# Moving the emission of the second half of the long-range attention behind two output projections

## The chip, the cores and the metric

The kernel runs on one core of a Trainium2 chip. A core has a matrix engine (PE, with its weight loads shown apart as PEld), a vector engine (DVE), a scalar engine (ACT), a general engine (POOL) and a queue engine (SP, SyncE) that here issues every DMA; sixteen DMA engines carry the transfers between the core's memory and the chip's main memory. The metric is the device time of one execution in microseconds, as the median of several runs; lower is better.

## What is computed

One layer of a hybrid encoder over a prompt of 2048 tokens and 32 sample tokens, with 1024 features. Two groups of attention heads work side by side: group A is a long-range differential attention over all earlier chunks, group B looks only at a band of nine chunks.

```
qa, ka, va, qb, kb, vb = split(rmsnorm(x) @ w_in)
oa = diff_attn(qa, ka, va)       # group A, 4 heads, chunk-causal over all keys
ob = band_attn(qb, kb, vb)       # group B, 8 heads, band of 9 chunks
h  = x + concat(rmsnorm(oa), rmsnorm(ob)) @ w_out
h  = h + relu(rmsnorm(h) @ w_up)**2 @ w_down
y  = rmsnorm(h + sigmoid(h @ w_gate) * (p @ w_proj))
```

Everything is float32. Each product is made of three matmuls in a reduced format: an operand is split in a high part (a rounded copy, made on ACT) and a low part (the rest, made on POOL or DVE), and the products high-high, high-low and low-high are summed (`mm3`, L216 to L222). `split` and `wunit` (L179 to L208) do this for each weight tile: a DMA load of 512 KB into `wr`, a copy on ACT into `wh`, a subtraction on POOL into `wl`.

## The kernel before

The tokens are cut in four blocks, 0 to 3: three of 512 and a last one of 544. Work is emitted in this order: the input projections; the first half of the group A attention (`attn_a` for the query pairs in `JA0`); the band attention (`attn_b`) in two parts; then, in `run` (from L1389), the stage around the change:

- the normalisation and the load of the attention output of block 0 (`onorm`, `oload`);
- the second part of the group A attention, `attn_a` for `JA1 = [(4, 5), (6, 7, 8)]`, that is, query pairs 4 to 7 and the sample tokens, whose outputs are read only by blocks 2 and 3;
- the output projection of block 0 (`outproj(0, ...)`), woven with the normalisation and load of block 1;
- the output projection of block 1, woven with the normalisation of block 0 for the MLP (`norms`, `cnorm`);
- the MLP of block 0, the MLP of block 1, the gate of block 1, and then everything for blocks 2, 0 and 3.

`outproj` (from L917) loops over eight column tiles d. Each d loads a weight tile of `w_out` (through `wunit`), loads a 256 KB tile `hd` of the input, makes 24 matmuls into `ops`, adds them to `hd` on DVE (L935), squares `hd` on ACT into `tmp` (L940) and stores `hd` to the scratch tensor `hS`. The tiles `hd`, `tmp`, `oraw` of `oload` and `tmp` of `cnorm` share one ring of four buffers, so that a load waits until an older tile is stored or used up. `cnorm` (from L945) reads `hS` back, scales it on DVE (L957) and splits it into `cH` and `cL`, the operands of the first MLP matmuls (`ups`).

`attn_a` (from L549) loops over four heads g. For each it loads a query tile (two DMAs for `q`), the keys (`ka`, for `JA1`'s first item two tiles in four DMAs) and a bias tile (`ba`), then works on each query pair of the item; a second pair has a `q` of its own. The loads of the first head need buffers of pools that are free once the input projections are done. The working tiles of `attn_a` lie where those of `attn_b` lay, and both use the same PSUM rings in the order in which they are emitted, so its computation comes after the last band attention.

No order is written out by hand for the engines. A list scheduler orders the instructions when the program is built: it keeps a timeline of its own, and gives each engine the earliest emitted instruction among those that are ready. What is emitted earlier thus goes first wherever both are ready, and what is emitted later fills the gaps. On the chip, each engine, SP among them, works through the list so made; an instruction that waits holds up those behind it. `tc.issue_after(x)` adds an edge that places what the block emits on x's engine behind x in that engine's list; it is an order of issue and no wait for x to end.

Of the kernel before, what the change touches and what calls it, by code (L numbers as in the profile page):

```python
# [76 lines left out]
JA1 = [(4, 5), (6, 7, 8)]  # L77
# [7 lines left out]
def drain(gen):  # L85
    for _ in gen:
        pass
# [13 lines left out]
def weave(main, side, step, i=0, n=1):  # L101
    for _ in main:
        if i % step == 0:
            for _ in range(n):
                next(side, None)
        i += 1
    drain(side)
# [37 lines left out]
class Kern:  # L145
# [44 lines left out]
    def wunit(self, src, shape, hi_eng="act", lo_eng="pool", pool=None):  # L190
        nc = self.nc
        if pool is None:
            raw = self.rawp.tile([P] + shape, F32, bufs=2, name="wr")
        else:
            raw = pool.tile([P] + shape, F32, tag="wr0", bufs=4, name="wr0")
        self.dma(raw, src)
        if self.pieces is not None:
            n = shape[0] // 2
            parts = []
            for x in range(2):  # L200
                parts.append(self.piece([n] + shape[1:]))
                self.split(*parts[x], raw[:, n * x : n * x + n], hi_eng, lo_eng)
            return tuple(Parts([p[i] for p in parts], n) for i in range(2))
        if pool is None:
            hi = self.wp.tile([P] + shape, F32R, tag="wh", bufs=3, name="wh")
            lo = self.wp.tile([P] + shape, F32R, tag="wl", bufs=3, name="wl")
        else:
            hi = pool.tile([P] + shape, F32R, tag="wh0", bufs=4, name="wh0")  # L208
            lo = pool.tile([P] + shape, F32R, tag="wl0", bufs=4, name="wl0")
        self.split(hi, lo, raw, hi_eng, lo_eng)  # L210
        return hi, lo
# [1177 lines left out]
    def run(self):  # L1389
        tc, nc, a = self.tc, self.nc, self.a  # L1390
        with ExitStack() as top:

            def opened(stack, name, bufs, space=None, side="left"):
                kw = {} if space is None else {"space": space}
                return stack.enter_context(
                    tc.tile_pool(name=name, bufs=bufs, side=side, reuse_waits="tile", **kw)
                )
# [17 lines left out]
            ps_o = opened(psx, "pso", 1, PSUM, "right")  # L1415
# [91 lines left out]
            self.qpool = opened(sq_, "ak", 1)  # L1507
            mz = mm
            sy = Rings((ps_s, "s"), (ps_t, "tp"), (ps_s, "s"), (ps_t, "tp"))
            with ExitStack() as x:  # L1510
                pool = opened(x, "a1", 1, side="right")
                self.kpool = Rings((self.qpool, "ka"), (self.qpool, "ka"), (Lean(pool, 1), "ka"))
                for js in JA1:
                    self.attn_a(js, pool, sy, sy, ps_o)
            self.nt = 4
            acc, cn, st = {}, {}, {}
            def norms(b, act, ps):
                self.colnorm(acc[b][0], b, 1.0 / D, wk, ps, "mm", self.rS)
                yield
                yield from self.cnorm(b, wk, act, cn)  # L1520
# [10 lines left out]
                        next(g, None)  # L1531
            drain(g)
            weave(self.outproj(1, wk, oa[1], mm, acc[1]), norms(0, actq, mm), 1, 1)
            up = Sized(opened(top, "uh", 20, side="right"), BLK)
            oxs = ExitStack()
            ox = opened(oxs, "ox", 1, side="right")
# [143 lines left out]
```

## Time and profile before

| what | value |
|---|---|
| median of 3 runs | 3037.97 us |
| lowest, highest | 3032.81, 3038.74 us |
| the profiled execution, its own time | 3036.97 us |
| span from its first to its last instruction | 3035.2 us |
| PE busy | 2936.1 us (97% of the span) |
| PEld, DVE, ACT, POOL busy | 85%, 60%, 58%, 62% |
| DMA moved | 528.50 MB, mean 174 GB/s |
| mean granted TensorE clock | 0.989 |

The profiled execution took 1.77 us more than its span, which is what lies around the first and the last instruction, and it ran 1.00 us under the median. A row of the timeline has its start, its duration, the engine, the line and the operation, and in brackets the idle time before it with what ended it. A row of the windows view has, for a stretch, the busy time of each engine with the number of instructions started (x), then the granted clock, the busy share of the DMA engines, and GB/s.

### The profile page before, as it was taken

The numbers are of one execution on the slowest core, as the hardware profiler recorded it, in microseconds if no ns is written. First come the engines' busy times: TensorE is split into PE (matmuls) and PEld (weight loads), VectorE is DVE, ScalarE is ACT, GpSimd is POOL, SyncE is SP. The second block draws the span as 40 slices with busy tenths as digits, with TensorE's granted clock in tenths as the row PEclk, the third lists the DMA queues.
The fourth block names the chain that finished last, engine by engine and source line by source line (L and its number), as shares of the span: only waits on it lengthen the run. The fifth ranks groups of instructions, "written<-read, shape, count | busy, mean of one in ns | idle before, by whom it ended". The sixth has DMA issues, their size and how long they took to land. (4 is left out here: it accounts for less than half of the span.)

```text
span 3035.2 us, 50381 instructions
## 1 busy us (share of the span) xinstructions
PE 2936.1 (97%) x17409; PEld 2590.1 (85%) x17409; DVE 1825.3 (60%) x4233; ACT 1746.3 (58%) x3234; POOL 1886.8 (62%) x2509
## 2 busy tenths in 40 slices
PE   7999999999999999999999999999899999999997
PEld 6788889999877888888888888779788888999997
DVE  5157564666655555666665666445677885677664
ACT  5256554777766665655565656454655555555455
POOL 3467775323456444756555655777687889787774
PEclk9999999999999999999999999999999999999999
DMA  9778766887877452645644443436433446323221
GB/s 310 263 223 247 238 226 208 264 245 216 247 250 220 149 158 84 197 151 160 210 135 138 143 146 103 160 137 229 154 108 119 153 142 240 127 91 119 100 101 54
DMA packets 297496, 528.50 MB, mean 174 GB/s; under 512 B 36557, under 2 KB 161521, under 8 KB 297241
## 3 DMA queue, kind: packets, MB, share of 16 engines
q1 hardware_dynamic: 297240, 525.28, 54.6%
q8 instruction: 138, 2.26, 0.3%
q14 instruction: 118, 0.96, 0.1%
HBM read 424.66 MB, written 104.45 MB: 174 GB/s over the span
## 5 line engine op out<-in xcount | busy, mean ns | idle before, releaser
L177 POOL TENSOR_TENSOR wl<-wr,wh 128x256 fp32r<-128x256 f32 x648 | 490.0, 789 | 241.5 <-ACT wh L182 224.0
L182 ACT ACTIVATE piece<-wr 128x512 fp32r<-128x512 f32 x406 | 245.9, 625 | 288.6 <-PE ups L221 136.8
L177 POOL TENSOR_TENSOR piece<-wr,piece 128x256 fp32r<-128x256 f32 x404 | 336.4, 860 | 91.2 <-ACT piece L182 83.9
L182 ACT ACTIVATE wh<-wr 128x1024 fp32r<-128x1024 f32 x228 | 240.4, 1056 | 195.9 <-PE ups L221 37.3
L167 POOL TENSOR_TENSOR wl<-wr,wh 128x256 fp32r<-128x256 f32 x264 | 203.1, 803 | 197.9 <-ACT wh L182 197.6
L220 PE MATMUL dps<-uh,piece 128*128 128x272 f32 (+1 forms) x768 | 246.6, 325 | 7.9 <-ACT piece L182 4.2
L167 POOL TENSOR_TENSOR piece<-wr,piece 128x256 fp32r<-128x256 f32 x280 | 238.0, 886 | 18.4 <-ACT piece L182 15.0
L222 PE MATMUL dps<-uh,piece 128*128 128x272 f32 (+1 forms) x768 | 247.1, 324 | 0.7 <-POOL piece L167 0.4
L221 PE MATMUL dps<-ul,piece 128*128 128x272 f32 (+1 forms) x768 | 247.5, 324 | 0.0
L220 PE MATMUL ups<-cs,piece 128*128 128x256 f32 (+1 forms) x864 | 245.5, 284 | 0.0
L222 PE MATMUL ups<-cs,piece 128*128 128x256 f32 (+1 forms) x864 | 245.5, 284 | 0.0
L221 PE MATMUL ups<-cs,piece 128*128 128x256 f32 (+1 forms) x864 | 245.3, 284 | 0.0
L220 PE MATMUL qps<-aH,wh 128*128 128x512 f32 (+1 forms) x640 | 226.2, 353 | 1.5 <-DVE ql L476 1.5
L221 PE MATMUL qps<-aL,wh 128*128 128x512 f32 (+1 forms) x640 | 226.7, 354 | 0.0
L222 PE MATMUL qps<-aH,wl 128*128 128x512 f32 (+1 forms) x640 | 226.3, 354 | 0.0
L639 ACT ACTIVATE e<-e,nm 128x128 f32<-128x128 f32 (+16 forms) x136 | 157.2, 1156 | 105.3 <-DVE nm L637 105.0
L1121 DVE TENSOR_TENSOR h<-h,dps 128x512 f32<-128x512 f32 x256 | 173.4, 682 | 70.2 <-PE dps L222 68.8
L1164 DVE TENSOR_TENSOR h<-h,dps 128x272 f32<-128x272 f32 (+1 forms) x384 | 189.0, 513 | 42.4 <-PE dps L222 42.0
L220 PE MATMUL dps<-uh,wh 128*128 128x512 f32 x512 | 205.5, 401 | 4.2 <-DVE h L1121 4.0
L220 PE MATMUL ups<-cH,wh 128*128 128x512 f32 x512 | 203.2, 398 | 3.5 <-ACT cH L182 3.5
L222 PE MATMUL ups<-cH,wl 128*128 128x512 f32 x512 | 202.8, 396 | 0.0
L221 PE MATMUL ups<-cL,wh 128*128 128x512 f32 x512 | 202.6, 396 | 0.0
(311 smaller groups left out, 9219.2 us busy)
## 6 DMA issues: line engine op xcount, KB each, us to landing
wr<-w_up SPq DMA_DIRECT2D x128, 512.0 KB, 3.5
wr<-w_down SPq DMA_DIRECT2D x128, 512.0 KB, 3.5
v<-vSa SPq DMA_DIRECT2D x64, 512.0 KB, 4.9
q<-qS SPq DMA_DIRECT2D x128, 256.0 KB, 5.6
wr<-w_qk SPq DMA_DIRECT2D x50, 512.0 KB, 5.3
ka<-kS SPq DMA_DIRECT2D x32, 512.0 KB, 8.6
wr<-w_out SPq DMA_DIRECT2D x32, 512.0 KB, 4.8
wr<-w_ple_gate SPq DMA_DIRECT2D x32, 512.0 KB, 3.5
```

Of the source, the lines that this page charges most:

```text
L167: nc.gpsimd.tensor_tensor(out[:, sl], a[:, sl], b[:, sl], op=op)
L177: nc.gpsimd.tensor_tensor(out[:, sl], a[:, sl], b[:, sl], op=op)
L182: nc.scalar.activation(hi, raw, AF.Copy)
L220: nc.tensor.matmul(ps, lh, rh, start=start and i == 0, stop=False)
L221: nc.tensor.matmul(ps, lh, rl, start=False, stop=False)
L222: nc.tensor.matmul(ps, ll, rh, start=False, stop=stop and i == n - 1)
L639: nc.scalar.activation(row, row, AF.Exp, bias=nmx, accum_out=z[:nr, m : m + 1])
L1121: nc.vector.tensor_tensor(hv, hv, ps, op=ALU.add)
L1164: nc.vector.tensor_tensor(hv, hv, ps, op=ALU.add)
```

## The change

The block that emits `attn_a` for `JA1` moves from ahead of `outproj(0)` to behind `outproj(1)`, and so behind the work woven with both. In the order of emission it is still ahead of the MLPs. Its instructions on SP, loads and stores, are placed behind the last weight load that was issued by `wunit`, for which `wunit` now keeps the load in `self.load`; at that point it is the load of `w_out`'s tile d = 7 for block 1.

```diff
-        self.dma(raw, src)
+        self.load = self.dma(raw, src)
...
             sy = Rings((ps_s, "s"), (ps_t, "tp"), (ps_s, "s"), (ps_t, "tp"))
-            with ExitStack() as x:
-                pool = opened(x, "a1", 1, side="right")
-                self.kpool = Rings((self.qpool, "ka"), (self.qpool, "ka"), (Lean(pool, 1), "ka"))
-                for js in JA1:
-                    self.attn_a(js, pool, sy, sy, ps_o)
             self.nt = 4
...
             weave(self.outproj(1, wk, oa[1], mm, acc[1]), norms(0, actq, mm), 1, 1)
+            with ExitStack() as x:
+                pool = opened(x, "a1", 1, side="right")
+                self.kpool = Rings((self.qpool, "ka"), (self.qpool, "ka"), (Lean(pool, 1), "ka"))
+                with tc.issue_after(self.load.ins):
+                    for js in JA1:
+                        self.attn_a(js, pool, sy, sy, ps_o)
             up = Sized(opened(top, "uh", 20, side="right"), BLK)
```

## The prediction

> **What bounds the kernel now.** I read the page first, then the windows view in five stretches, then in tens of microseconds where the first view loses something, then PE's waits there, and last the timelines of SP, DVE, ACT and PE around the longest wait.
>
> ```profile
> span 3035.2 us, 50381 instructions
> PE 2936.1 (97%) x17409; PEld 2590.1 (85%) x17409; DVE 1825.3 (60%) x4233; ACT 1746.3 (58%) x3234; POOL 1886.8 (62%) x2509
> ```
> ```profile
> 800.00:1000.00 200.00, 185.27 (x868) 151.22 (x868) 112.73 (x317) 127.83 (x239) 109.90 (x157) 0.95 0.78 237
> 1000.00:1900.00 900.00, 894.26 (x4607) 753.09 (x4606) 544.65 (x1383) 548.04 (x905) 500.13 (x708) 1.00 0.49 147
> ```
>
> PE is busy for 97% of the span, so the time is PE's work plus what PE loses. The change removes no matmul and adds none. From 1000 to 1900 us, where the moved attention is computed beside the MLPs, PE idles 900 - 894.3 = 5.7 us at clock 1.00; there is next to nothing to gain there. From 800 to 1000 us, the two output projections and the start of the MLP, it idles 14.7 us at clock 0.95. That stretch decides.
>
> ```profile
> 820.00:830.00 10.00, 10.00 (x50) 8.28 (x50) 6.74 (x22) 8.29 (x17) 6.27 (x11) 1.00 1.04 234
> 830.00:840.00 10.00, 9.87 (x52) 8.18 (x50) 1.77 (x7) 2.23 (x5) 3.81 (x7) 1.00 1.08 269
> 840.00:850.00 10.00, 5.52 (x13) 4.29 (x14) 3.78 (x12) 5.83 (x10) 6.91 (x10) 0.67 0.75 260
> 850.00:860.00 10.00, 10.00 (x50) 8.39 (x50) 5.80 (x14) 6.98 (x12) 7.47 (x11) 0.99 0.75 220
> ...
> 870.00:880.00 10.00, 7.21 (x25) 5.53 (x24) 6.08 (x18) 6.63 (x13) 5.26 (x8) 0.70 0.74 243
> ...
> 910.00:920.00 10.00, 10.00 (x51) 8.42 (x50) 6.09 (x13) 4.18 (x9) 8.55 (x11) 1.00 0.68 200
> 920.00:930.00 10.00, 10.00 (x52) 8.28 (x51) 3.14 (x11) 6.06 (x11) 5.04 (x9) 1.00 1.03 295
> 930.00:940.00 10.00, 8.44 (x40) 6.46 (x40) 6.20 (x14) 6.70 (x13) 9.91 (x14) 1.00 0.60 194
> 940.00:950.00 10.00, 8.89 (x40) 6.11 (x38) 5.54 (x14) 5.36 (x10) 5.36 (x7) 1.00 1.01 331
> 950.00:960.00 10.00, 6.77 (x25) 4.87 (x26) 5.26 (x18) 5.49 (x12) 1.86 (x2) 0.80 1.05 273
> 960.00:970.00 10.00, 9.95 (x42) 7.97 (x41) 6.01 (x17) 9.41 (x19) 6.84 (x11) 0.86 0.45 140
> ```
> ```profile
> PE ops L220 <- ACT wh L182: 4.6, 1, 4.6
> PE ups L220 <- ACT cH L182: 3.5, 2, 2.4
> PE ops L220 <- DMA oraw<-oT: 2.5, 1, 2.5
> ```
>
> Count matmuls, not busy time: behind an idle stretch the clock is low and matmuls last longer, which busy time hides. An undisturbed ten microseconds (850 to 860) start 50, so one is worth 0.20 us. By that measure there are three holes:
>
> - **Hole 1**, 840 to 850: 13 matmuls, 37 short: 7.4 us, for 4.48 us of idle time.
> - **Hole 2**, 870 to 880: 25 short: 5.0 us.
> - **Hole 3**, 930 to 970: 147 of 200, 53 short: 10.6 us, for 40 - 34.05 = 5.95 us of idle time, so 1.78 us lost for each idle one.
>
> The low clock behind a hole is in these prices. The Trainium skill ("TensorE: Matmul & The Clock Gate", Part 1) has the clock halved after an idle window of about 3.4 us and restored after as long a busy one; by that rule hole 1 would cost 4.6 + 1.7 = 6.3 us, and hole 2, idle for 2.8 us, need not throttle at all. The row of 870 to 880 grants 0.70 after the shorter idle time, so I go by the counted matmuls; with the rule's price in both places the sum below would be lower by 0.7 us.
>
> **What makes hole 1.** SP's list before it, and what its loads do to others:
>
> ```profile
> 818.10 2.93 SPq L158 DMA_DIRECT2D q<-qS  x4
> 821.20 0.48 SPq L158 DMA_DIRECT2D bb<-dbb  x1
> 821.72 2.54 SPq L158 DMA_DIRECT2D ka<-kS  x4
> 824.31 0.59 SPq L158 DMA_DIRECT2D ba<-dba  x1
> 825.14 0.57 SPq L158 DMA_DIRECT2D q<-qS  x1
> 826.61 0.37 SPq L158 DMA_DIRECT2D vbt<-vSb  x1
> 827.54 2.43 SPq L158 DMA_DIRECT2D q<-qS  x1
> 830.17 1.45 SPq L158 DMA_DIRECT2D hS<-hd  x2
> 833.87 0.34 SPq L158 DMA_DIRECT2D hd<-x_t  x1
> ```
> ```profile
> 841.35 0.69 DVE L935 TENSOR_TENSOR hd<-hd,ops 128x512 f32<-128x512 f32 x1 [6.78 <-DMA hd<-x_t]
> ```
>
> Nine of these DMAs are the first head of the moved attention: two `q` of the four at 818.10 (the other two belong to the band attention), four `ka`, one `ba`, and the two `q` at 825.14 and 827.54. The sizes in the page's list of DMA issues (`q` 256 KB, `ka` two of 512 and two of 256, `ba` 128) give 2688 KB, 2.75 MB. At the 234 and 269 GB/s of the rows from 820 to 840, where the DMA engines are full (1.04, 1.08), that is 2.75 MB / 251 GB/s = **10.9 us of all DMA engines**, and SP issues nothing of the projection between 818 and 830. Two stores of `hd` wait behind them, then `hd<-x_t` for d = 2. It goes at 833.87, and DVE gets it at 841.35, 7.5 us later. The same load after the burst:
>
> ```profile
> hd<-x_t SPq DMA_DIRECT2D x1, 256.0 KB, 2.9
> ba<-dba SPq DMA_DIRECT2D x1, 128.0 KB, 11.1
> ```
>
> lands in 2.9 us. So it comes 4.6 us late by the transfer alone, and the chain DVE add, ACT square, ACT copy of the next weights, PE follows: PE idles 4.6 us (the first of PE's waits above). A late tile here goes through to PE one for one.
>
> **The change part by part.** Moving the emission removes nothing and takes the nine DMAs out of 818 to 830. The computation need not follow, since it begins only behind the last band attention:
>
> ```profile
> 1180.00:1190.00 10.00, 1.30 (x6) 1.00 0.24 74
> ```
>
> These are its first six QK matmuls (the windows view of the tile `s`; after 750 us no earlier row has any). With loads at 920 instead of 820 us they are still over 200 us early, so attention loses nothing, and its priority against the MLPs is unchanged. Its stores on SP come later than either place: nothing.
>
> *Hole 1* goes: -7.4 us. Bounds: -7.4, and 0 if `hd` has another brake. I take -7.4, because the 4.6 us of late landing explain the whole wait. What is late next is hole 2, a wait for `oraw<-oT` (the third of PE's waits), 30 us later; I leave it at 5.0 us.
>
> *The new place* is SP's list right behind the last `w_out` load:
>
> ```profile
> 913.71 0.38 SPq L158 DMA_DIRECT2D wr<-w_out  x1
> ...
> 917.56 0.53 SPq L158 DMA_DIRECT2D wr<-w_up  x1
> 918.21 0.45 SPq L158 DMA_DIRECT2D hS<-hd  x1
> 921.30 0.33 SPq L158 DMA_DIRECT2D tmp<-hS  x1
> 922.72 0.33 SPq L158 DMA_DIRECT2D hd<-x_t  x1
> ```
> ```profile
> tmp<-hS SPq DMA_DIRECT2D x1, 256.0 KB, 8.1
> ```
>
> The nine rank above the first `w_up` load (the MLP is emitted later) and below `hS`, `tmp` and `hd`. In the present list the lower-ranking `w_up` got in ahead of `hS`, `tmp` and `hd`, so these were not yet ready then; I expect the nine to get in there too. The queue they join is no emptier: `tmp<-hS` at 921.30 already takes 8.1 us, and the row of 920 to 930 has the DMA engines full (1.03). Room comes at 930 to 940 (0.60, 4 us free). Behind the nine stand `hS<-hd` of d = 4, the `tmp` loads that make `cH`, and `hd` of d = 5 to 7: the chain on which hole 3 waits (`ups` for `cH`). POOL gets the bias tile's memset, which waits for `ba` (11.1 us in flight above), with the `wl` subtractions of `w_up` behind it.
>
> The added idle time is bounded by 0 (the nine go behind the critical loads, or into free room) and 10.9 us (all of their transfer passes through). The nearest row is hole 1: the same bytes, ahead of the same kind of chain, made 4.48 us. I take that, at hole 3's 1.78: 4.48 x 1.78 = +8.0 us.
>
> Sum: -7.4 + 8.0 = **+0.6 us**. On the profiled execution's own 3036.97 us (span 3035.2 and 1.77 around it) that is 3037.6; the median of the runs stands 1.0 us above that execution, so I predict **3038.6 us**.
>
> **The rivals.** All times are on the median's scale.
>
> - *Hidden*: `hS`, `tmp` and `hd` come first in the new list, or the nine fall into the free 4 us and what is left is behind `cH`. For it: the higher rank of these three, and 917 to 920 has SP time. Against: the order of the list above. It gives 3038.0 - 7.4 = 3030.6; if hole 2 closes as well, since projection 1 starts earlier against the band attention's loads, 3025.6.
> - *The whole burst passes through*, the case on the slower side. The place is SP between `w_out` d = 7 and `tmp<-hS`; all nine stand ahead of the loop `hS`, `tmp`, `hd`, which has no reserve left, as PE already idles for it. The row of 910 to 920 (0.68) leaves about 1 us free from 917 on, of the 10.9, so 9.9 us of idle time x 1.78 = 17.6, less 7.4: +10.2, or 3048.2. It decides for slower once the added idle time passes (7.4 + 6.1) / 1.78 = 7.6 us. Against it: hole 1 took only 4.48 from the same burst, under some cover. The Trainium skill ("DMA: Bandwidth & Descriptors", Queues, rings and completion order) has each DMA engine consume its descriptors in ring order, by which a moved burst holds up whatever stands behind it for its full length; the 11.1 us of `ba` agree.
> - *The change doesn't do what it says*: the nine move, yet hole 1 stays, because the band attention's own loads (the other two `q`, `bb` and `vbt` above) or the ring of four buffers hold `hd` too. Then 3038.0 + 8.0 = 3046.0. Against it: the 2.9 us landing directly behind the burst.
>
> **How the numbers follow.** Forecast 0.42, hidden 0.25, whole burst 0.25, hole 1 stays 0.08. About 0.2% of the time, 6.1 us, is what a measurement of this kernel can tell from no change. The forecast lies within it; hidden is faster; the last two are slower. So faster 0.25, same 0.42, slower 0.33. The range must take in most of the hidden case and of the whole burst: 3027 to 3049 leaves out the double closing of holes 1 and 2 and a burst dearer than 10.9 us, together some 0.2. The forecast's own range is 3032 to 3044.
>
> **What would show it.** Right: no `ka` or `ba` on SP before the sixteenth `w_out` load; no wait of `ops` for `wh` over 2 us in outproj(0), and 50 matmuls in each of its ten microseconds; `tmp<-hS` and `hd<-x_t` behind the nine with landings over 10 us; the start of the MLP with some 4 to 5 us more idle time and a clock under 0.9. Wrong: landings of `tmp` still near 8 us (hidden), or a wait of 8 us and more at the first `ups` (whole burst). A different loss behind 1000 us, where PE now loses 5.7 us in 900, would mean that the list scheduler dealt the later order anew, for which I have no term.

## The result and the profile after

The changed kernel took 3043.95 us (median of 20 runs, 3035.37 to 3049.41), the kernel before 3038.01 us in the runs beside them (20 runs, 3032.06 to 3044.39). The ratio is **1.0023, 95% interval 1.0016 to 1.0029**: slower by 7.0 us (4.9 to 8.8; the two medians by themselves differ by 5.9), about the 6.1 us that the prediction took for the least that can be told from no change. The range on record holds the time; the forecast itself was 0.6 us slower than before, so 6.4 us are missing from its sum.

The page of the changed kernel, its span and the busy time of the engines; then, from the windows view, the two stretches that the prediction compared:

```profile
span 3042.0 us, 50377 instructions
...
PE 2942.3 (97%) x17409; PEld 2594.4 (85%) x17409; DVE 1827.3 (60%) x4233; ACT 1743.7 (57%) x3234; POOL 1899.7 (62%) x2509
```
```profile
800.00:1000.00 200.00, 180.99 (x847) 147.79 (x847) 116.01 (x321) 129.09 (x245) 111.82 (x155) 0.94 0.78 234
1000.00:1900.00 900.00, 895.20 (x4599) 753.62 (x4597) 542.66 (x1374) 543.95 (x898) 509.61 (x714) 1.00 0.49 147
```

The same 17409 matmuls. From 800 to 1000 us PE starts 847 of them where it started 868: 21 fewer, at 0.20 us each 4.2 us. From 1000 to 1900, where the moved attention is computed, it starts 8 fewer, 1.6 us, less than executions of like kernels differ there (4599 to 4635 in all the kernels of this study). So the loss lies where it was looked for, and the later emission costs the attention next to nothing.

The windows of ten microseconds of the changed kernel show what went and what came (after the PE column come PEld, DVE, ACT and POOL, then the granted clock, the DMA share and GB/s):

```profile
840.00:850.00 10.00, 10.00 (x51) 8.51 (x51) 4.11 (x14) 6.38 (x13) 8.79 (x13) 1.00 0.60 181
...
900.00:910.00 10.00, 9.71 (x47) 7.57 (x46) 4.54 (x11) 6.70 (x11) 8.76 (x11) 1.00 0.86 260
910.00:920.00 10.00, 8.51 (x40) 6.52 (x39) 3.37 (x11) 5.01 (x10) 2.44 (x4) 1.00 1.05 231
920.00:930.00 10.00, 6.65 (x27) 5.31 (x27) 3.97 (x12) 4.74 (x8) 7.61 (x12) 0.83 1.05 262
...
950.00:960.00 10.00, 6.18 (x22) 5.07 (x23) 4.58 (x12) 4.10 (x9) 1.91 (x2) 0.66 0.99 275
960.00:970.00 10.00, 7.80 (x30) 5.38 (x29) 8.89 (x25) 8.28 (x17) 3.94 (x4) 0.79 0.38 115
```

Hole 1 is closed: 51 matmuls from 840 to 850 where there were 13. In its place stands a **new hole from 900 to 930**: 47 + 40 + 27 = 114 of 150, 36 short, 7.2 us, with the DMA engines full (1.05). The hole at the start of the MLP is still there. Not all of the new hole comes from the loads: in the three kernels below that take them past 1000 us, the same rows have 139, 143 and 137 of 150. By the hundred, PE starts 452 matmuls from 800 to 900 (427 before) and 397 from 900 to 1000 (443 before).

How the new hole comes about is read from four engines. SP's timeline of the changed kernel, from the last `w_out` load on:

```profile
904.54 0.33 SPq L158 DMA_DIRECT2D wr<-w_out  x1
904.92 0.62 SPq L158 DMA_DIRECT2D q<-qS  x1
905.65 0.66 SPq L158 DMA_DIRECT2D hd<-x_t  x1
906.37 0.61 SPq L158 DMA_DIRECT2D q<-qS  x1
907.02 2.54 SPq L158 DMA_DIRECT2D ka<-kS  x4
909.61 0.59 SPq L158 DMA_DIRECT2D ba<-dba  x1
912.07 0.33 SPq L158 DMA_DIRECT2D hS<-hd  x1
912.51 0.37 SPq L158 DMA_DIRECT2D tmp<-hS  x1
912.97 0.38 SPq L158 DMA_DIRECT2D hd<-x_t  x1
914.98 1.75 SPq L158 DMA_DIRECT2D q<-qS  x2
918.72 0.34 SPq L158 DMA_DIRECT2D wr<-w_up  x1
```

Seven of the nine loads go ahead of `hS`, `tmp` and `hd`, two behind, all nine ahead of `w_up`. DVE's timeline of the same kernel:

```profile
921.77 1.04 DVE L957 SCALAR_TENSOR_TENSOR tmp<-tmp,g_mlp_s,rl 128x512 f32<-128x512 f32 x1 [5.84 <-DMA tmp<-hS]
...
923.70 0.48 DVE L808 CUSTOM_DVE_ANT_0 eb<-sb,bb 128x320 f32<-128x320 f32 x1
```

DVE stands for 5.84 us until the `tmp` that was issued at 912.51 is there, 9.3 us later. What is queued behind it on DVE is the band attention's softmax at L808, which has nothing to do with `tmp`. PE's timeline has the other end of it:

```profile
924.25 1.23 PE L805 MATMUL sb<-kbt,q 128*128 128x320 f32 x4 [3.35 <-DVE stb L808]
...
953.82 1.22 PE L220 MATMUL ups<-cH,wh 128*128 128x512 f32 x2 [4.99 <-ACT cH L182]
```

and POOL's timeline shows the memset of the bias tile that waits for `ba`, with the subtraction for the next weights behind it at 920.16:

```profile
920.06 0.14 POOL L336 MEMSET ba<- 64x64 f32 x1 [5.79 <-DMA ba<-dba]
```

PE's waits from 810 to 1000 us in the changed kernel:

```profile
PE sb L805 <- DVE stb L808: 5.6, 4, 3.3
PE ups L220 <- ACT cH L182: 5.0, 1, 5.0
PE ops L220 <- ACT oact L182: 2.6, 2, 1.9
PE ops L221 <- DVE oact L188: 2.0, 1, 2.0
```

The wait of `ops` for `wh` (4.6 us before) is gone, the wait of `sb` for DVE went from 0.9 us to 5.6, that of `ups` for `cH` from 3.5 to 5.0, and in third place stands a wait of `ops` for `oact`, which the list of before has not: hole 2 in another shape.

### The profile page after: what moved, and what is told of

The parts are those of the page before. It is cut to its first block, busy times and chain, and to the rows that moved or that the text cites. A ratio compares the mean times of both kernels' runs of the same rounds, so it can differ in the third digit from the quotient of the medians.

```text
span 3042.0 us, 50377 instructions
## 1 busy us (share of the span) xinstructions
PE 2942.3 (97%) x17409; PEld 2594.4 (85%) x17409; DVE 1827.3 (60%) x4233; ACT 1743.7 (57%) x3234; POOL 1899.7 (62%) x2509
## 5 line engine op out<-in xcount | busy, mean ns | idle before, releaser
L167 POOL TENSOR_TENSOR piece<-wr,piece 128x256 fp32r<-128x256 f32 x280 | 236.1, 878 | 17.6 <-ACT piece L182 14.2
```

The source lines that it names most:

```text
L167: nc.gpsimd.tensor_tensor(out[:, sl], a[:, sl], b[:, sl], op=op)
```

## The experiments

**Theory 1**: the loss belongs to the nine loads; their price is what their place in SP's list makes it, since the loop of `hS`, `tmp` and `hd` stands behind them. **Theory 2**, the rival: it belongs to the new order of emission, which deals the work of the other engines anew. All ratios are to the kernel before on the same chip.

**The loads alone.** The emission of before; only SP's instructions of the attention are held behind the last `w_out` load.

```diff
                 for js in JA1:
                     self.attn_a(js, pool, sy, sy, ps_o)
+                held = [i for i in nc.cur_bb.bb.instructions[n0:] if i.engine == mybir.EngineType.SP]
...
+            for i in held:
+                tc.add_manual_dep(i, self.load.ins.name, ...)
             up = Sized(opened(top, "uh", 20, side="right"), BLK)
```

> The emission of the kernel before, with only the SP instructions of the moved attention held behind the last w_out load. If the nine early loads make the loss by where they stand (theory 1), this is as slow as the change: 3041 to 3047 us, with a hole of about 30 to 40 missing matmuls between 900 and 930 us, and no wait of 4 us in outproj(0). If the loss comes from the new order of emission on the other engines (theory 2), it goes back to about 3038 us.

Measured: 3040.83 us to 3034.56, ratio **1.0021** (1.0010 to 1.0031), the loss of the whole change. SP's timeline of this kernel has all nine in one piece, with `hd` behind them:

```profile
900.05 1.87 SPq L158 DMA_DIRECT2D q<-qS  x2
901.97 2.55 SPq L158 DMA_DIRECT2D ka<-kS  x4
904.56 0.61 SPq L158 DMA_DIRECT2D ba<-dba  x1
905.22 1.69 SPq L158 DMA_DIRECT2D q<-qS  x2
907.70 0.34 SPq L158 DMA_DIRECT2D hd<-x_t  x1
```

DVE's timeline has that `hd`, its windows view the price on PE:

```profile
918.98 0.69 DVE L935 TENSOR_TENSOR hd<-hd,ops 128x512 f32<-128x512 f32 x1 [11.76 <-DMA hd<-x_t]
```
```profile
910.00:920.00 10.00, 2.14 (x10) 1.49 (x9) 1.02 (x4) 0.24 (x1) 2.88 (x5) 0.76 1.06 234
```

`hd` is there 11.3 us after its issue, nearly the 10.9 us of DMA time that the prediction worked out for the nine; DVE waits 11.76 us, PE 7.9 us (its list of waits). From 900 to 930 PE starts 52 + 10 + 38 = 100 matmuls, 50 short, where 30 to 40 were expected. The loads are enough to make the loss. (This one profiled execution, with a span of 3034.0 us, is about 5 us faster than the median of its kernel's runs; it shows the mechanism, and the ratio shows the size.)

**The move alone.** The change without the edge, so that the list scheduler places the loads by their rank.

```diff
-                with tc.issue_after(self.load.ins):
-                    for js in JA1:
-                        self.attn_a(js, pool, sy, sy, ps_o)
+                for js in JA1:
+                    self.attn_a(js, pool, sy, sy, ps_o)
```

> The emission moved as in the change, but the loads are free to go early, and the list again has the nine between 820 and 835 us, now with hS and hd of d = 0 to 2 ahead of the last six of them. Theory 1: no hole between 900 and 930; hole 1 at 840 smaller than the 7.4 us of before, since hd for d = 2 is in front of part of the burst: 3032 to 3038 us. Theory 2: as slow as the change, 3042 to 3046 us.

Measured: ratio 1.0001 (0.9993 to 1.0009), no change. The scheduler puts the loads back to where they were, but since they now rank lower, `hS` and `hd` get in between, as SP's timeline shows:

```profile
825.80 1.89 SPq L158 DMA_DIRECT2D ka<-kS  x3
828.50 1.05 SPq L158 DMA_DIRECT2D hS<-hd  x2
829.60 0.42 SPq L158 DMA_DIRECT2D hd<-x_t  x1
...
831.52 3.23 SPq L158 DMA_DIRECT2D ka<-kS  x1
```

From 840 to 860 PE starts 40 + 41 matmuls there, against 13 + 50 in the kernel before. Of the two parts of the change, the edge makes the loss; theory 2 falls.

**Later, in two places.** The attention is emitted inside the first MLP, so that its SP instructions stand behind another weight load: the fourth of `w_up` in one kernel, the last of the second chunk in the other. `second()` holds the moved block; the earlier place has `range(1)` for `range(3)`.

```diff
-            with ExitStack() as x:
-                pool = opened(x, "a1", 1, side="right")
...
                 if b == 0:
                     next(m)
...
+                    for _ in range(3):
+                        next(m)
+                    second()
```

> The emission and the loads behind the fourth w_up load of the first MLP, about 942 us, in the middle of hole 3. The SP list is that of the change up to the last w_out load. Theory 1: the hole at 900 to 930 goes (-7.2 us against the change), hole 3 at 940 to 970 grows by some 4 to 8 us: 3038 to 3045 us. Theory 2: no difference from the change, 3042 to 3046 us.

> The same, behind the second chunk's weights, about 985 us, where the DMA engines are busy for 0.3 to 0.5 of the time and PE has the MLP to do. Theory 1: neither hole 1 nor the hole at 900 to 930, hole 3 as before: 7 to 10 us under the change, 3033 to 3037 us, faster than the kernel before. Theory 2: no difference from the change, 3042 to 3046 us.

Measured: behind the fourth `w_up`, 1.0022 (1.0010 to 1.0034), as slow as the change. Behind the second chunk, 3032.69 us and **0.9988** (0.9978 to 0.9998), faster than before and the best version found. PE's longest wait in the first of them, by the list of its waits:

```profile
PE ups L220 <- ACT cH L182: 9.8, 1, 9.8
```

There the nine loads (936.70 to 955.7 us) stand among the last `tmp` loads, so the price is paid at the first matmul of the MLP. In the kernel with the latest place they go at 1000.68 to 1006.6 us, and its windows from 900 to 1000 us are:

```profile
900.00:1000.00 100.00, 93.30 (x433) 74.95 (x432) 49.93 (x144) 63.58 (x118) 60.49 (x86) 0.97 0.68 210
```

433 matmuls against 397 in the change. From 800 to 1000 us it starts 886, where the kernel before starts 868.

**The loads late, the emission of before.** As in the first experiment, with the edge to that later load.

> The emission of the kernel before, the SP instructions of the moved attention held behind the weights of the MLP's second chunk. Theory 1: the emission is of no account, the same as the late experiment, 0.12% under before (0.9978 to 0.9998). If moving the emission has a price or a gain of its own, the two differ by it.

Measured: 0.9993 (0.9984 to 1.0002). Its interval overlaps that of the late kernel above for the most part: again the place of the loads counts, and the order of emission does not show.

**Part of the loads late.** The change, with the four `ka` and the `ba` held to the late place and only the four `q` (1024 of 2688 KB) behind the last `w_out` load.

> The change, but of the nine early loads only the four q (1.0 MB) stand behind the last w_out load; ka and ba (1.7 MB) wait until the weights of the MLP's second chunk, as in the late experiment. Theory 1 (the bytes that stand ahead of the loop hS, tmp, hd make the loss): about 1.0 of 2.75 MB of the burst's price, 2 to 4 us over the late experiment, so 3035 to 3039 us where before has 3038. If one load is enough to hold up the loop (a matter of order, not of bytes), as slow as the change, +5 us or more.

Measured: 1.0001 (0.9992 to 1.0011), between the change and the late place, as a price that grows with what stands there would have it; its interval overlaps that of the late place and ends just under that of the change.

**More bytes, in both places.** The change, and the late kernel, with each `ka` load issued a second time into a scratch tensor that nobody reads (1.57 MB more).

```diff
                     self.dma(kt[64 * hl : 64 * hl + 64, :, :n], src[:, :, c0 : c0 + n])
+                    if g == 0 and js[0] == 4:
+                        self.dma(self.again[hl, :, :, c0 : c0 + n], src[:, :, c0 : c0 + n])
```

> The change, with the four ka loads of the first head issued once more, into a scratch tensor that nobody reads: 1.57 MB more in the burst behind the last w_out load. Theory 1: the hole at 900 to 930 grows by 5 to 11 us, so 3049 to 3055 us. If the burst were absorbed there and the loss came from elsewhere: as the change, 3044 us.

> The late experiment with the same 1.57 MB more, behind the weights of the MLP's second chunk. Theory 1: free there, within 2 us of the late experiment (0.12% under before). If bytes cost the same wherever they are moved, 5 to 11 us over it.

Measured: late 0.9988 (0.9980 to 0.9997), so 57% more bytes are free there. Behind `w_out`, 3039.36 us and 1.0010 (1.0001 to 1.0019): **not slower than the change, where 3049 us and more were expected**. That was a miss. A price by the bytes of the whole burst does not hold. The extra loads changed the list: `hS`, `tmp` and `hd` now go at 913.93, behind seven transfers and ahead of six. By the sizes of the loads, 2560 KB stand ahead of them, against 2176 KB in the change: 18% more, not 57%. PE's waits are spread over the band attention (8.7 us in six waits of `sb`, none above 2.8; this profiled execution, at 3044.57 us, was the slowest of its kernel). The bytes were changed and the order with them, so this pair does not tell them apart.

**Order without the loop behind.** The change, with the edge to the last `tmp` load in place of the last `w_out` load, so that nothing of the loop stands behind the nine, though they still go before 960 us; beside it the change itself again.

```diff
-                with tc.issue_after(self.load.ins):
+                with tc.issue_after(self.back.ins):     # cnorm's last load of tmp
```

> The change, with the nine loads behind the last two loads of tmp (the ones that make the last column tiles of cH) in place of the last w_out load: some 40 us later than in the change, some 55 us earlier than in the latest place tried, and with nothing of the loop hS, tmp, hd behind them. If the price is that loop standing behind the bytes (theory 1): no wait of ups for cH above 6 us, no wait of DVE for hd or tmp above 5 us after the nine, the ten microseconds from 900 to 960 as in the kernel with the latest place (about 200 matmuls), and a ratio of 0.998 to 1.000 to the kernel before. If instead any 2.75 MB put on the DMA engines before about 960 us cost what they cost in the change, whatever stands behind (rival: plain bandwidth): some 35 to 45 matmuls fewer between 900 and 1000 than in the kernel with the latest place, and 1.001 to 1.003.

> The change itself, unaltered, timed beside the kernel with the loads behind the last tmp on the same chip. Expected 1.0023 of the kernel before (1.0016 to 1.0029 was measured). Its profile should repeat the two new things, a hole of some 35 matmuls between 900 and 930 us and DVE waiting over 4 us for tmp or hd; if the hole lies elsewhere in this execution, the place of the loss varies from one execution to the next and only its sum counts.

Measured: behind the last `tmp` 3039.22 us, **1.0009** (1.0000 to 1.0018); the change again 3046.58 us, 1.0044 (1.0029 to 1.0060), dearer than the first time (the two intervals just touch), with the same picture. SP's timeline of the first:

```profile
944.48 1.17 SPq L158 DMA_DIRECT2D tmp<-hS  x2
945.70 1.33 SPq L158 DMA_DIRECT2D q<-qS  x2
947.07 6.04 SPq L158 DMA_DIRECT2D ka<-kS  x4
```

and its windows from 900 to 1000 us:

```profile
900.00:1000.00 100.00, 89.76 (x412) 71.61 (x411) 49.83 (x141) 59.96 (x111) 57.35 (x81) 0.95 0.80 231
```

By the list of PE's waits, `ups` waits 2.5 us for `cH`, where it was 5.0 in the change, as theory 1 had it; but 412 matmuls are 21 fewer than in the latest place (433), 4.2 us, and the ratio, 0.0021 or 6.4 us over that place, is not the 0.998 to 1.000 expected. Neither side came out whole: of the price of the place behind `w_out` (0.0035 over the latest place, or 0.0056 by the repeat on the same chip), taking the loop out from behind the loads removes 0.0014 or 0.0035, two to three fifths. Some 4 to 6 us stay while the DMA engines are full (1.06 from 950 to 960, 1.05 from 960 to 970 in this kernel), with the weights for the MLP, `kbt` and `vbt` behind. The repeat of the change has both marks, a DVE wait for `tmp` of 6.0 us and 34 matmuls short from 900 to 930 (45, 45, 26); its `ups` waits 6.7 us for `cH`, and it starts 392 matmuls from 900 to 1000. The long wait for `tmp` is no sure mark, though: it reaches 4.7 us in the latest place and 5.6 in the kernel behind the last `tmp`, there at 940 us, ahead of the nine.

## Why the prediction was right and wrong

The kernel with the loads in the latest place, with and without the extra bytes, and the one that moves the loads alone there, measure what hole 1 was worth: 0.9988, 0.9988 and 0.9993, on average 0.9990, or **-3.1 us** (the medians alone give -1.7 to -2.3, and the widest ends of the three intervals are -6.7 and +0.6). The change is at 1.0023, so the place behind `w_out` costs 0.0033, or **+10.1 us** (by the repeat of the change, 1.0044, it would be 16). The forecast had -7.4 and +8.0: its gain is too large and its price too small, and both errors point the same way, so nothing cancelled. The range held because it is 22 us wide, to take in two rivals on opposite sides; of the times on record the nearest to the 3043.95 measured is the 3046.0 of the third rival, whose mechanism the next lines refute.

*Hole 1 goes, and nothing else made it*: right. Its windows are full, the wait of `ops` for `wh` is gone, and the third rival (hole 1 stays) is refuted.

*"What is late next is hole 2 [...] I leave it at 5.0 us"*: **this step failed**. PE comes to the second projection earlier, and so does the operand that it needs there, but PE waits for it again and is held up once or twice more behind it. The wait in the kernel before and its first piece in the change:

```profile
874.73 0.79 PE L220 MATMUL ops<-oact,wh 128*128 128x512 f32 x1 [2.50 <-DMA oraw<-oT]
```
```profile
869.29 0.50 PE L220 MATMUL ops<-oact,wh 128*128 128x512 f32 x1 [1.94 <-ACT oact L182]
```

In the change 0.29 and 0.62 us more follow by 872; in the latest place it is 2.57 and 0.57. The windows from 860 to 880 of the kernel before, of the change, and of the kernel with the latest place:

```profile
860.00:880.00 20.00, 17.21 (x76) 14.07 (x75) 11.41 (x32) 12.27 (x23) 11.51 (x17) 0.85 0.87 287
```
```profile
860.00:880.00 20.00, 17.06 (x68) 13.21 (x67) 13.93 (x31) 11.81 (x23) 8.93 (x11) 0.83 0.74 241
```
```profile
860.00:880.00 20.00, 16.06 (x63) 11.66 (x62) 12.85 (x29) 11.76 (x22) 9.93 (x12) 0.83 0.77 251
```

8 and 13 matmuls fewer: hole 2 grows by 1.6 and 2.6 us, where the forecast left it alone, and the wait changed its name, from `oraw<-oT` to `oact`, which is made from it. From 800 to 900 the change gains 25 matmuls, 5.0 us, not 37. From 800 to 1000 the three kernels with the loads past 1000 us start 886, 894 and 887, against 868 before: 3.6 to 5.2 us, which goes with the 3.1 of the runs. That hole 2 takes all of the missing gain is not shown.

*The added price*, 4.48 us of idle time x 1.78 = 8.0: right in kind, and too small. From 900 to 1000 us the change idles 100 - 87.38 = 12.62 us, 6.66 more than before (94.04 busy), and starts 46 matmuls fewer, 9.2 us: 1.38 for each idle one. So the idle time was taken too low and the factor too high. That hole 1 had more cover than this place would explain the first; no run tests it. The price lies between the forecast's and that of the rival in which the whole burst passes through (17.6 us), and by the repeat (16) close to the latter.

*Where the price is paid*: right in the main, by the counts. Set beside the kernel before, the change seems to pay from 900 to 930 and to be no worse from 930 to 970 (150 matmuls against 147). But the kernel before has hole 1, and the price is what separates the change from the latest place, where hole 1 is gone too. From 950 to 1000 us the change and the latest place have:

```profile
950.00:1000.00 50.00, 43.67 (x192) 35.05 (x193) 27.80 (x85) 34.25 (x68) 25.18 (x36) 0.86 0.57 171
```
```profile
950.00:1000.00 50.00, 47.02 (x227) 38.83 (x226) 25.10 (x75) 34.27 (x65) 28.21 (x42) 0.97 0.55 165
```

That is 35 matmuls fewer (the repeat of the change has 184, the other two kernels with late loads 226 and 233). From 900 to 950 it is 205 and 208 in the two executions of the change, against 208, 220 and 204: little. So most of the price falls at the start of the MLP, where `ups` waits for `cH` (5.0 and 6.7 us, against 1.7, 2.3 and 2.7) and the clock is 0.86 against 0.97, as forecast. What the forecast missed is the detour: `sb` of the band attention waits for DVE (5.6 and 6.0 us, against 2.8, 2.5 and 2.2) while DVE waits for `tmp`. It followed data only (`tmp`, `cH`, `ups`) and not what is queued behind the waiting instruction on DVE. The place is not fixed either: the kernel that moves the loads alone pays at 910 to 920, where `hd` is late, and its `ups` waits 0.6 us for `cH`. On POOL the forecast named the memset that waits for `ba`; it waited 5.8 us.

*The signs named*: there is no `ka` or `ba` before the sixteenth `w_out` load, as forecast. At the start of the MLP the clock falls to 0.66 and 0.79, as forecast, but from 930 to 970 PE idles 7.2 us against 5.95, not 4 to 5 more. The landings misled. The list of DMA issues for 904 to 930 us of the changed kernel gives last the median time from issue to landing:

```profile
hd<-x_t SPq DMA_DIRECT2D x3, 256.0 KB, 6.9
...
tmp<-hS SPq DMA_DIRECT2D x2, 256.0 KB, 8.0
```

The `tmp` with 8.0 us, which the prediction had put down as the sign of the hidden case (it was 8.1 before), is the one issued at 925.54. For the one at 912.51, on which DVE stood, the view has no landing; DVE had it 9.3 us after its issue. It is also issued behind a burst that SP takes from 904.92 to 910.20 us to get out. Time to landing leaves out the time that a load stands in SP's list.

Of the Trainium skill, the rule that each DMA engine consumes its descriptors in ring order ("DMA: Bandwidth & Descriptors", Queues, rings and completion order) was cited for the dear rival. The kernel that moves the loads alone agrees with it: `hd`, right behind the nine, took 11.3 us against 2.9 after the burst in the kernel before. But the ratio of that kernel is the change's: not every microsecond of lateness reached PE, which idled 7.9 us there.

**What stays open**: how much of the price is order and how much bandwidth. With the loop behind the loads it is 1.0023 and 1.0044, with the loop ahead 1.0009; but there the loads also go 40 us later. A price by the bytes ahead of the loop roughly fits the kernel with `q` alone (1024 KB, a third of the way from the late place to the change) and fails in the one with 2560 KB; no run changed the bytes and kept the order.

## What to carry to other kernels

Price a prefetch by what is queued behind it, on the DMA queue first and then on each engine that waits for one of the delayed tiles: here the loads were the same, and their place made 0.9988, 1.0009, 1.0022 or 1.0023 (1.0044 in the repeat). To find where a price is paid, compare with a kernel that lacks the old stall too, here the one with the loads in the latest place. When you close a stall, do not book its whole length: find what the engine meets next, and whether that comes any earlier; here hole 1 was booked at 7.4 us and gave about 3. And move a burst with slack of hundreds of microseconds not just behind the next weights, but on to the first stretch where the DMA engines have room (0.49 busy from 1000 us on) and the engine that bounds the kernel has nothing to wait for.

## What the runs showed of the hardware that was not expected

- 57% more bytes cost nothing at 1000 us (both 0.9988), and a first 2688 KB cost 10 us at 904.
- SP itself is held up while the DMA engines are full. A single `ka` issue took it 0.6 us at 907 in the change (DMA share 0.86) and 3.23 at 831.52 in the kernel with the move alone (1.06); a single `q` 2.43 at 827.54 in the kernel before (1.04). Longer rows hold waits between the issues as well: of the 6.04 us for four `ka` behind the last `tmp`, 3.1 are a wait that the profile puts down to the landing of the 2 MB load `h<-hS`; of the 7.03 for two `q` behind the fourth `w_up`, 5.6. Why SP waits for that load is not shown. What stands behind is issued late before it is late.
- The length of an idle time alone does not set the clock. In the change, PE's timeline has 1.94, 0.29 and 0.62 us of idle time between 867 and 872, and the clock from 870 to 880 is 0.66; the 3.35 us in one piece before 924.25 leave 0.83 from 920 to 930 and 1.00 from 930 to 940. The Trainium skill's idle window of about 3.4 us ("TensorE: Matmul & The Clock Gate", Part 1) doesn't account for the first of these. The values 0.83 and 0.66 come back in row after row of ten microseconds. The first 128x512 matmuls of `ups` in the change (930 to 965) take 389 ns at the median and up to 796, about twice as long; if the low clock is half the full one, 0.83 is 3.4 us of it, and 0.66 twice that.
- One profiled execution doesn't size an effect of 5 us by its span. Up to 800 us the change's two profiled executions started 4875 and 4879 matmuls, but the kernels of this study, whose work up to there hardly differs, lie between 4863 and 4894: 31 matmuls, 6 us.
